# Sums of squares from the feature-major input and the decay chain one block earlier, in a fused transformer block

## The chip, the cores and the metric

The kernel runs on one core of one Trainium2 chip. A time is the device time of one execution in microseconds (us); the profiled execution also has a span, from its first to its last instruction. Weights and activations are float32 in memory.

## What is computed

One block of a hybrid network on 256 tokens of 2048 features: a token mixer (a gated MLP with spatial gating, and a chunked gated linear attention, GLA), cross attention over a memory, and a convolutional feed-forward layer, each with RMS norms around it. What the change touches is the start of the mixer:

```python
def rmsnorm(x, g):
    return x * rsqrt(mean(x * x, -1) + EPS) * g
h = rmsnorm(x, pre_norm_mix)
z_sg, q, k, v, og, g_lr, m_a, m_b = split(h @ w_in)
u, vs = split(gelu(z_sg), 2)
y_a = spatial_gating(u, layernorm(vs, sg_ln_g, sg_ln_b), sg_w, sg_b)
gate_logit = g_lr @ gla_w_gate2 + gla_b_gate
log_a = maximum(log_sigmoid(gate_logit) / 16, -1)
bcum = cumsum(log_a)                  # in chunks of 64 tokens
q_in, k_in = q * exp(bcum), k * exp(-bcum)
```

## The kernel before

**Products in high and low parts.** A float32 operand is split into a high part, a cast on ScalarE (`split_half`, L89), and a low part, a subtraction on VectorE (L90); TensorE multiplies high by high, low by high and high by low. Weights arrive in tiles of 1 MB (`raw`, three buffers, loaded from SP's queue) and are split in pieces of 128 x 1024; there are four buffers of high and four of low parts, so TensorE can have at most four pieces ahead. In a block with tokens on the output's partitions (`tok_block`, L117) a piece feeds 12 matmuls of 512 columns; with features there (`feat_block`, L143), 8 of 512 and 8 of 256. The products accumulate in PSUM, with six tiles tagged `mm` and two tagged `aux`.

**Order.** Most of the kernel is ordered by a scheduler that works on a simulated time line and takes instructions roughly in program order where they are ready. Inside `tc.manual_schedule` the order is as written. The list `later` holds small pieces of work; `tok_block` runs one of them after each piece but the first, `feat_block` after each piece (`step`), and `flush` runs the rest.

**The first projection** (L399 to L453) is written out by hand. It multiplies the input `xT`, which is in memory feature-major (features on partitions), with the second half of the spatial gating's weights, in eight units of two feature blocks. A unit takes 24 matmuls. For each unit the input is scaled by the norm's gain and split (`gain_x`, L372), the weights are split, and TensorE runs. The factor rstd of each token is applied behind the product, so it is needed only when the projection's result leaves PSUM.

**Sums of squares.** For rstd the token-major rows of x are loaded as well, in eight pieces of 128 x 512 (`load_x`, L357), squared on ScalarE with a sum (`square_x`, L362, L366), summed on VectorE, and raised to the power -1/2 on POOL (`rstd_of`, L150). `row_bcast` (L176) multiplies the identity by rstd and puts a row of it on all partitions with two matmuls (`rbc`).

**Low-rank gate.** Sixteen matmuls with the rank-16 weights (L452) follow, then ScalarE and VectorE make `glr` of the result (L455 to L462).

**After that.** `sg_v` takes the first projection out of PSUM with a Gelu (L467), and layer norm over it (L476 to L483) runs on VectorE. Then come two blocks of the projection for `u` (`tok_block`, L549 and L552, matmuls at L106 to L108) with a Gelu each (`sg_u`, L470). Within the first, `gate` (L493) runs four times with two matmuls each, and `decay` (L503): absolute value, Exp, Ln and subtractions. Within the second, `cums` (L509) runs a scan along the tokens and builds exponents, and `powers` (L528) makes two exponentials for each of four heads; `powers` for heads 1 to 3 stand in the q and k blocks (L582). Those (L579 to L603, matmuls at L137 to L141) use the powers on VectorE behind their products; `gating` (L533, matmuls `sps` at L537) uses layer norm's result and `u`.

Of the kernel before, what the change touches and what calls it, by code (L numbers as in the profile page):

```python
# [11 lines left out]
F32 = mybir.dt.float32  # L12
F32R = mybir.dt.float32r
AF = mybir.ActivationFunctionType
# [3 lines left out]
P = 128  # L18
# [6 lines left out]
H = 4  # L25
# [19 lines left out]
def block_kernel(ctx: ExitStack, tc: tile.TileContext, a, out):  # L45
# [269 lines left out]
    with ExitStack() as mix:  # L315
# [20 lines left out]
        with ExitStack() as st2:  # L336
            xp0 = pool(st2, "sp0", side="right")

            gmix = xp0.tile([P, KD], F32, name="gmix")
            xt = [xp0.tile([P, 2, S], F32, name=f"xt_{i}") for i in range(KD // 2)]  # L340
            wgr = xp0.tile([P, KD, 16], F32, name="glr_raw")
            wg = xp0.tile([P, KD, 5, 16], F32R, name="wg")
            gl1 = xp0.tile([80, S], F32, name="gl1")
            gh1 = xp0.tile([48, S], F32R, name="gh1")
            g2 = uu[1][0:96, :]
            xh, ss4s, rs = {}, {}, []

            def load_xt(k, n, eng=nc.sync):
                eng.dma_start(out=xt[k // 2][:, k % 2:k % 2 + n, :], in_=a["xT"][:, k:k + n, :])

# [5 lines left out]

            def load_x(i):  # L357
                t, n = divmod(i, 4)
                xh[i] = xp0.tile([P, 512], F32, tag="xh", bufs=3, name=f"x0_{t}_{n}")
                nc.sync.dma_start(out=xh[i], in_=a["x"][t * P:(t + 1) * P, n * 512:(n + 1) * 512])  # L360

            def square_x(i):  # L362
                t, n = divmod(i, 4)
                if n == 0:
                    ss4s[t] = stat.tile([P, 4], F32, tag="ss4", name=f"ss4_mix_{t}")
                nc.scalar.activation(out=uu[0][:, 0:512], in_=xh[i], func=AF.Square, accum_out=ss4s[t][:, n:n + 1])  # L366
                if n == 3:
                    ss = stat.tile([P, 1], F32, tag="ss", name=f"ss_mix_{t}")
                    nc.vector.reduce_sum(out=ss, in_=ss4s[t], axis=AX.X)
                    rs.append(rstd_of(ss, 1.0 / D, f"mix_{t}", const.tile([P, 1], F32, name=f"r_mix_{t}")))  # L370

            def gain_x(k):  # L372
                split_psum(hT[:, k, 0, :], hT[:, k, 1, :], xt[k // 2][:, k % 2, :], scale=gmix[:, k:k + 1])

            def later_loads(i):
                if i == 3:
                    nc.sync.dma_start(out=ident, in_=a["eye"])
# [6 lines left out]
                if i == 4:  # L384
                    nc.sync.dma_start(out=wgr, in_=a["w_glr"])
                    nc.sync.dma_start(out=g2, in_=a["gate2"])
                if i == 6:
# [5 lines left out]
                    nc.vector.tensor_tensor(out=gate2[64:96, :], in0=g2[64:96, :], in1=gate2[64:96, :].bitcast(F32),  # L393
                                            op=ALU.subtract)
                    nc.sync.dma_start(out=lng, in_=a["sg_ln_g"].partition_broadcast(P))
                if i == 7:
                    nc.sync.dma_start(out=lnb, in_=a["sg_ln_b"].partition_broadcast(P))

            first = []  # L399
            with tc.manual_schedule():  # L400
# [12 lines left out]
                pss = [[mm_psum(f"sg_{n}_{t}") for t in range(NT)] for n in (2, 3)]  # L413
                nx = 0
                for i in range(KD // 2):
                    if 1 <= i < KD // 2 - 2:
                        load_xt(2 * i + 4, 2)
                        load_unit()
# [17 lines left out]
                    for j in sorted(xh):  # L436
                        if j >= nx:
                            square_x(j)
                    nx = len(xh)
                    for j in {2: (0, 1), 3: (2,), 4: (3, 4), 5: (5,), 6: (6, 7)}.get(i, ()):  # L440
                        load_x(j)
                    later_loads(i)
                    for k in (2 * i, 2 * i + 1):
                        c = slice(k % 2 * 512, (k % 2 + 1) * 512)
                        for n, (hi, lo) in enumerate(hl):
                            for j, (part, w) in enumerate(((0, hi), (1, hi), (0, lo))):
                                for t in range(NT):
                                    nc.tensor.matmul(pss[n][t], hT[:, k, part, t * P:(t + 1) * P], w[:, c],
                                                     start=k == 0 and j == 0, stop=k == KD - 1 and j == 2)
                ps = mm_psum("glr")  # L450
                for k in range(KD):
# [22 lines left out]
        for n, ps in enumerate(pss):  # L474
            sg_v(ps, n + 2)
        for t in range(NT):  # L476
            mv = stat.tile([P, 2], F32, tag="mv", name=f"mv_{t}")
# [7 lines left out]
        with ExitStack() as st2:  # L485
# [5 lines left out]
            nc.gpsimd.memset(keep[:, :, 0:1], 0.0)  # L491

            def gate(i):  # L493
                gps = aux_psum(f"gate_{i}")
                for j in range(2):
# [4 lines left out]
                nc.scalar.activation(out=la[:, 2 * i:2 * i + 2, :], in_=gv, func=AF.Abs)  # L500
                nc.vector.tensor_scalar_min(mn[:, 2 * i:2 * i + 2, :], gv, 0.0)

            def decay():  # L503
                nc.scalar.activation(out=la, in_=la, func=AF.Exp, scale=-1.0)
                nc.scalar.activation(out=la, in_=la, func=AF.Ln, bias=1.0)
                nc.vector.tensor_tensor(out=la, in0=mn, in1=la, op=ALU.subtract)
                nc.vector.tensor_scalar(out=la, in0=la, scalar1=1.0 / 16.0, scalar2=-1.0, op0=ALU.mult, op1=ALU.max)
# [39 lines left out]

            later += [partial(gate, i) for i in range(4)] + [decay]
            sg_u(tok_block(a["w_sg"], 0, hT, KD, "sg"), 0)  # L549
            flush()  # L550
            later += [cums, partial(powers, 0)]
            ps = tok_block(a["w_sg"], 1, hT, KD, "sg")  # L552
# [8 lines left out]
        with ExitStack() as st:  # L561
# [454 lines left out]
```

## Time and profile before

| what | value |
|---|---|
| three runs, median | 1662.66 us (1661.40 to 1663.66) |
| the profiled execution, its own time | 1661.93 us |
| its span | 1660.20 us |
| TensorE busy | 1646.9 us |
| VectorE busy | 1042.1 us |
| ScalarE busy | 846.1 us |
| mean granted TensorE clock | 0.999 |

Rows of a timeline give the start, the busy time, the engine (PE is TensorE, ACT ScalarE, DVE VectorE, SP the engine that issues most transfers), the line of the kernel, the operation, its output and inputs, shapes and a count; in brackets stands the idle time before it and what ended it. The end of a matmul is modelled: its busy time overlaps the next one's, so starts are to be compared, not busy times. One float32 matmul counts as two records.

### The profile page before, as it was taken

The page shows a single profiled execution, that of the slowest core. Times are in us where ns is not written, and L with a number is a line of the kernel's source. Part 1 is how long each engine was busy: PE and PEld are TensorE (multiplying, and loading weights), DVE is VectorE, ACT ScalarE, POOL GpSimd, SP SyncE. Part 2 cuts the span into 40 slices and gives each one's busy share as a digit, 9 for nine tenths or more (in the row PEclk, how much of TensorE's full clock was granted, in tenths as well). Part 3 has the DMA queues.
Part 4 walks back from the last instruction along what each step waited for, and adds up shares of the span by engine and source line. Part 5 has one row for each costly group of instructions (what it writes and reads, how often), then busy time and mean ns, then how long its engine had stood idle before and what let it go on. Part 6 is the DMA issues. An engine that isn't in the chain of part 4 may idle for free.

```text
span 1660.2 us, 20835 instructions
## 1 busy us (share of the span) xinstructions
PE 1646.9 (99%) x8086; PEld 1374.8 (83%) x8086; DVE 1042.1 (63%) x1394; ACT 846.1 (51%) x1182; POOL 39.8 (2%) x128
## 2 busy tenths in 40 slices
PE   9999999999999999999999999999999999999998
PEld 7788888888888888888888888888888888888886
DVE  5777645555454545465766877877777787444444
ACT  6774444444444444455655756555555555344332
POOL 0100000000000000000002000000000000000000
PEclk9999999999999999999999999999999999999999
DMA  9545455445555554585542555555555555555553
GB/s 344 221 160 177 177 186 172 176 176 177 186 194 178 182 198 178 187 333 215 204 177 105 202 193 187 181 200 178 190 191 182 195 181 216 190 187 193 179 199 103
DMA packets 49139, 317.52 MB, mean 191 GB/s; under 512 B 5552, under 2 KB 6192, under 8 KB 12304
## 3 DMA queue, kind: packets, MB, share of 16 engines
q1 hardware_dynamic: 48752, 315.93, 53.4%
q8 instruction: 63, 1.03, 0.2%
q14 instruction: 36, 0.29, 0.1%
q10 hardware_dynamic: 288, 0.27, 0.0%
HBM read 314.08 MB, written 2.10 MB: 190 GB/s over the span
## 4 chain that ended last, share of the span: by engine, by line
PE 95%; DMA 2%; ACT 1%; issue 1%; DVE 1%; SPq 0%; DVEq 0%; POOLq 0%; POOL 0%; ACTq 0%
PE up L137 18%; PE up L138 10%; PE ffn L108 5%; PE ffn L107 5%; PE ffn L106 5%; PE m L108 4%; PE m L107 4%; PE m L106 4%; PE p L108 3%; PE p L106 3%; PE p L107 3%; PE mix L108 2%; PE mix L106 2%; PE og L107 2%; PE v L108 2%; PE og L106 2%
## 5 line engine op out<-in xcount | busy, mean ns | idle before, releaser
L90 DVE TENSOR_TENSOR lo<-raw,hi 128x1024 fp32r<-128x1024 f32 (+1 forms) x567 | 689.5, 1219 | 460.9 <-ACT hi L89 456.7
L89 ACT CAST hi<-raw 128x1024 fp32r<-128x1024 f32 (+1 forms) x568 | 590.5, 1043 | 534.4 <-PE ffn L107 133.6
L137 PE MATMUL up<-fT,hi 128*128 128x512 f32 x1320 | 467.3, 394 | 0.4 <-DVE fT L210 0.4
L138 PE MATMUL up<-fT,lo 128*128 128x256 f32 x1320 | 373.1, 283 | 0.0
L137 PEld LDWEIGHTS up<-fT,hi 128*128 128x128 f32 x1320 | 247.9, 188 | 54.3 <-DVE fT L210 0.7
L138 PEld LDWEIGHTS up<-fT,lo 128*128 128x128 f32 x1320 | 248.1, 188 | 3.9
L108 PE MATMUL ffn<-lo,act 128*128 128x512 f32 x352 | 140.1, 399 | 0.0
L107 PE MATMUL ffn<-hi,act 128*128 128x512 f32 x352 | 138.7, 394 | 0.0
L106 PE MATMUL ffn<-hi,act 128*128 128x512 f32 x352 | 138.0, 392 | 0.0
L893 ACT COPY hd<-up 128x256 f32<-128x256 f32 x88 | 32.7, 373 | 137.0 <-PE up L141 137.0
L106 PE MATMUL m<-hi,hT 128*128 128x512 f32 x256 | 101.4, 396 | 0.0
L108 PE MATMUL m<-lo,hT 128*128 128x512 f32 x256 | 101.3, 396 | 0.0
L107 PE MATMUL m<-hi,hT 128*128 128x512 f32 x256 | 101.1, 395 | 0.0
L894 DVE TENSOR_TENSOR hd<-up,hd 128x256 f32<-128x256 f32 x88 | 37.4, 425 | 72.4 <-ACT hd L893 72.4
L107 PEld LDWEIGHTS ffn<-hi,act 128*128 128x128 f32 x352 | 66.1, 188 | 17.2
L106 PEld LDWEIGHTS ffn<-hi,act 128*128 128x128 f32 x352 | 66.1, 188 | 15.7
L108 PEld LDWEIGHTS ffn<-lo,act 128*128 128x128 f32 x352 | 66.1, 188 | 15.3
L107 PEld LDWEIGHTS m<-hi,hT 128*128 128x128 f32 x256 | 48.1, 188 | 11.4
L108 PEld LDWEIGHTS m<-lo,hT 128*128 128x128 f32 x256 | 48.1, 188 | 11.4
L106 PEld LDWEIGHTS m<-hi,hT 128*128 128x128 f32 x256 | 48.1, 188 | 11.2
L897 ACT ACTIVATE cv<-hd,cols 128x256 f32<-128x256 f32 x88 | 52.7, 602 | 0.3
L106 PE MATMUL v<-hi,hT 128*128 128x512 f32 x128 | 51.1, 399 | 0.0
(301 smaller groups left out, 2480.1 us busy)
## 6 DMA issues: line engine op xcount, KB each, us to landing
raw<-in_w_up SPq DMA_DIRECT2D x88, 1024.0 KB, 4.8
raw<-in_w_dn SPq DMA_DIRECT2D x44, 1024.0 KB, 4.8
raw<-in_w_v SPq DMA_DIRECT2D x16, 1024.0 KB, 4.8
raw<-in_w_og SPq DMA_DIRECT2D x16, 1024.0 KB, 4.8
raw<-in_w_ma SPq DMA_DIRECT2D x16, 1024.0 KB, 4.8
raw<-in_w_mb SPq DMA_DIRECT2D x16, 1024.0 KB, 4.8
raw<-in_w_pb SPq DMA_DIRECT2D x16, 1024.0 KB, 4.8
raw<-in_w_o SPq DMA_DIRECT2D x16, 1024.0 KB, 4.9
```

The costliest lines, as they stand in the source:

```text
L89: nc.scalar.copy(out=hi, in_=raw)
L90: (eng or nc.vector).tensor_tensor(out=lo, in0=raw, in1=hi.bitcast(F32), op=ALU.subtract)
L106: nc.tensor.matmul(ps, xh, wh, start=first, stop=False)
L107: nc.tensor.matmul(ps, xl, wh, start=False, stop=False)
L108: nc.tensor.matmul(ps, xh, wl, start=False, stop=last)
L137: nc.tensor.matmul(*big, start=k == 0, stop=False)
L138: nc.tensor.matmul(*small, start=False, stop=False)
L893: nc.scalar.copy(out=hd[:, 2:], in_=ps[:, S:2 * S])
L894: nc.vector.tensor_tensor(out=hd[:, 2:], in0=ps[:, 0:S], in1=hd[:, 2:], op=ALU.add)
L897: nc.scalar.activation(out=cv, in_=hd[:, 2:], func=AF.Identity, scale=cols[:, w0 + 2:w0 + 3], bias=cols[:, C_CB + j:C_CB + j + 1])
```

## The change

- The eight loads of token rows go. Squares are taken of `xT` itself, two feature blocks at a time, and added up on VectorE into `acc`; at the last feature block the two halves are added, and two matmuls with `acc` as the stationary operand and two columns of ones give each token's sum on its partition (`token_rstd`). One operation on VectorE and one power on POOL make both columns of rstd.
- `xT` lies in one tile; from the loop it is loaded in transfers of four, four and two feature blocks instead of two each.
- The rank-16 weights and the gate's weights are loaded a unit earlier and cast a unit earlier, identity and columns are loaded a unit later.
- Layer norm moves from before the first `u` block into the second.
- The four `gate` steps run in one, behind the third piece of the first `u` block, with PSUM tiles of the `mm` kind, and hold them until `decay`; the minimum with zero is fused into the subtraction. `decay`, `cums` and all four `powers` follow in the first block; TensorE's order in that block is as written.

```diff
-            xt = [xp0.tile([P, 2, S], F32, name=f"xt_{i}") for i in range(KD // 2)]
+            xt = xp0.tile([P, KD, S], F32, name="xt")
+            acc = xp0.tile([P, 2, S], F32, name="acc")
...
-            def load_x(i):
...
-                nc.sync.dma_start(out=xh[i], in_=a["x"][t * P:(t + 1) * P, n * 512:(n + 1) * 512])
...
             def square_x(i):
...
-                nc.scalar.activation(out=uu[0][:, 0:512], in_=xh[i], func=AF.Square, accum_out=ss4s[t][:, n:n + 1])
...
+                sq = acc if i == 0 else xp0.tile([P, 2, S], F32, tag="sq", bufs=2, name="sq")
+                nc.scalar.activation(out=sq, in_=xt[:, 2 * i:2 * i + 2, :], func=AF.Square)
+                if i > 0:
+                    nc.vector.tensor_tensor(out=acc, in0=acc, in1=sq, op=ALU.add)
+
+            def token_rstd():
+                nc.vector.tensor_tensor(out=acc[:, 0, :], in0=acc[:, 0, :], in1=acc[:, 1, :], op=ALU.add)
+                tot = aux_psum("tot")
+                for t in range(NT):
+                    nc.tensor.matmul(tot[:, 2 * t:2 * t + 2], acc[:, 0, t * P:(t + 1) * P], ones[:, 0:2],
+                                     start=True, stop=True)
+                ms = stat.tile([P, NT], F32, tag="ms2", name="ms_mix")
+                nc.vector.tensor_scalar(out=ms, in0=tot[:, 0:2 * NT:2], scalar1=1.0 / D, scalar2=EPS,
+                                        op0=ALU.mult, op1=ALU.add)
+                nc.gpsimd.tensor_tensor(out=rr, in0=ms, in1=neg_half, op=ALU.pow)
...
                     if 1 <= i < KD // 2 - 2:
-                        load_xt(2 * i + 4, 2)
+                        if i % 2:
+                            load_xt(2 * i + 4, min(4, KD - 2 * i - 4))
                         load_unit()
...
-                    for j in {2: (0, 1), 3: (2,), 4: (3, 4), 5: (5,), 6: (6, 7)}.get(i, ()):
-                        load_x(j)
+                    square_x(i)
                     later_loads(i)
                     for k in (2 * i, 2 * i + 1):
+                        if k == KD - 1:
+                            token_rstd()
...
-        for t in range(NT):
+        def layer_norm(t):
...
             def gate(i):
-                gps = aux_psum(f"gate_{i}")
+                gps = mm_psum(f"gate_{i}")
...
-                nc.vector.tensor_scalar_min(mn[:, 2 * i:2 * i + 2, :], gv, 0.0)
+                gvs.append(gv)
 
             def decay():
                 nc.scalar.activation(out=la, in_=la, func=AF.Exp, scale=-1.0)
                 nc.scalar.activation(out=la, in_=la, func=AF.Ln, bias=1.0)
-                nc.vector.tensor_tensor(out=la, in0=mn, in1=la, op=ALU.subtract)
+                for i, gv in enumerate(gvs):
+                    part = la[:, 2 * i:2 * i + 2, :]
+                    nc.vector.scalar_tensor_tensor(out=part, in0=gv, scalar=0.0, in1=part, op0=ALU.min, op1=ALU.subtract)
...
-            later += [partial(gate, i) for i in range(4)] + [decay]
-            sg_u(tok_block(a["w_sg"], 0, hT, KD, "sg"), 0)
+            def gates():
+                for i in range(4):
+                    gate(i)
+
+            later += [lambda: None, gates, decay, cums] + [partial(powers, q) for q in range(H)]
+            with tc.manual_schedule(engines={mybir.EngineType.PE}):
+                ps = tok_block(a["w_sg"], 0, hT, KD, "sg")
             flush()
-            later += [cums, partial(powers, 0)]
+            sg_u(ps, 0)
+            later += [partial(layer_norm, t) for t in range(NT)]
             ps = tok_block(a["w_sg"], 1, hT, KD, "sg")
...
-                if h < H - 1:
-                    later.insert(0, partial(powers, h + 1))
```

## Rows read from the trace of the kernel before

**Rows 1.** The page's first part: busy us, share of the span, instructions

```profile
PE 1646.9 (99%) x8086; PEld 1374.8 (83%) x8086; DVE 1042.1 (63%) x1394; ACT 846.1 (51%) x1182; POOL 39.8 (2%) x128
```

**Rows 2.** TensorE's timeline, first projection, two starts 26 repeats apart

```profile
7.96 1.09 PE L448 MATMUL sg<-hi,hT 128*128 128x512 f32 x4
...
44.36 1.09 PE L448 MATMUL sg<-hi,hT 128*128 128x512 f32 x4
```

**Rows 3.** TensorE's timeline, the last unit of the first projection

```profile
45.29 0.63 PE L448 MATMUL sg<-lo,hT 128*128 128x512 f32 x2
46.24 1.19 PE L448 MATMUL sg<-hi,hT 128*128 128x512 f32 x4 [0.32 <-ACT hi L89]
47.79 0.73 PE L448 MATMUL sg<-lo,hT 128*128 128x512 f32 x2 [0.36 <-DVE lo L90]
48.36 1.09 PE L448 MATMUL sg<-hi,hT 128*128 128x512 f32 x4
```

**Rows 4.** TensorE's timeline, end of the second u block and first q block

```profile
100.47 0.40 PE L107 MATMUL sg<-hi,hT 128*128 128x512 f32 x1
101.07 0.51 PE L108 MATMUL sg<-lo,hT 128*128 128x512 f32 x1 [0.20 <-DVE lo L90]
101.41 0.39 PE L106 MATMUL sg<-hi,hT 128*128 128x512 f32 x1
...
112.30 1.05 PE L537 MATMUL sps<-vv,sgw 128*128 128x128 f32 x8
113.78 0.49 PE L137 MATMUL q<-hT,hi 128*128 128x512 f32 x1 [0.42 <-ACT hi L89]
115.03 0.39 PE L138 MATMUL q<-hT,lo 128*128 128x256 f32 x1 [0.76 <-DVE lo L90]
115.26 0.39 PE L137 MATMUL q<-hT,hi 128*128 128x512 f32 x1
```

**Rows 5.** ScalarE to 56 us: a wait (total, times, longest), a timeline row

```profile
ACT uu L366 <- DMA x<-in_x: 8.6, 5, 2.6
...
45.15 3.88 ACT L89 CAST hi<-raw 128x1024 fp32r<-128x1024 f32 x4
```

**Rows 6.** VectorE's timeline: the scan

```profile
95.48 4.42 DVE L510 TENSOR_TENSOR_SCAN mn<-keep,la 128x2048 f32<-128x2048 f32 x1
```

**Rows 7.** ScalarE's timeline from the Ln to the casts of the q block

```profile
86.78 1.92 ACT L505 ACTIVATE la<-la 128x2048 f32<-128x2048 f32 x1
...
102.56 1.28 ACT L530 ACT_TABLE_LOAD   x1
...
105.95 1.03 ACT L89 CAST hi<-raw 128x1024 fp32r<-128x1024 f32 x1
106.89 3.90 ACT L531 ACTIVATE E<-E 128x1024 f32<-128x1024 f32 x4
110.81 1.28 ACT L472 ACT_TABLE_LOAD   x1
...
112.69 1.03 ACT L89 CAST hi<-raw 128x1024 fp32r<-128x1024 f32 x1
```

**Rows 8.** Groups of one shape to 126 us: busy us, mean ns | idle before

```profile
L366 ACT ACTIVATE uu<-x 128x512 f32<-128x512 f32 x8 | 5.1, 632 | 8.7 <-DMA x<-in_x 8.6
L90 DVE TENSOR_TENSOR lo<-raw,hi 128x1024 fp32r<-128x1024 f32 x37 | 44.2, 1220 | 15.2 <-ACT hi L89 15.1
L501 DVE TENSOR_SCALAR mn<-gate 128x512 f32<-128x512 f32 x4 | 2.7, 687 | 1.4 <-ACT la L500 1.4
L506 DVE TENSOR_TENSOR la<-mn,la 128x2048 f32<-128x2048 f32 x1 | 2.3, 2293 | 2.6 <-ACT la L505 2.6
```

**Rows 9.** Busy time by stretch: length, PE, PEld, DVE, ACT, POOL, clock, DMA

```profile
6.15:45.52 39.37, 39.37 (x168) 31.71 (x168) 24.93 (x35) 26.63 (x50) 1.65 (x2) 1.00 1.02 376
```

**Rows 10.** Timeline: the first u block's first matmul, the last step to glr

```profile
56.40 0.48 PE L106 MATMUL sg<-hi,hT 128*128 128x512 f32 x1
...
65.66 0.41 DVE L462 TENSOR_TENSOR glr<-gl,gh 16x256 fp32r<-16x256 f32 x1
```

More of the change, by code (lines that the diff above doesn't have):

```diff
@@ L344, in block_kernel @@
             gh1 = xp0.tile([48, S], F32R, name="gh1")
+            rr = const.tile([P, NT], F32, name="r_mix")
+            rs = [rr[:, t:t + 1] for t in range(NT)]
             g2 = uu[1][0:96, :]
-            xh, ss4s, rs = {}, {}, []
             def load_xt(k, n, eng=nc.sync):
-                eng.dma_start(out=xt[k // 2][:, k % 2:k % 2 + n, :], in_=a["xT"][:, k:k + n, :])
+                eng.dma_start(out=xt[:, k:k + n, :], in_=a["xT"][:, k:k + n, :])
             def load_unit(parts=((slice(0, 2), slice(0, 2)),)):
@@ L355, in load_unit @@
                     nc.sync.dma_start(out=first[i][:, n, k, :], in_=a["w_sgv"][i, :, n, k, :])
-            def load_x(i):
-                t, n = divmod(i, 4)
-                xh[i] = xp0.tile([P, 512], F32, tag="xh", bufs=3, name=f"x0_{t}_{n}")
-                nc.sync.dma_start(out=xh[i], in_=a["x"][t * P:(t + 1) * P, n * 512:(n + 1) * 512])
             def square_x(i):
-                t, n = divmod(i, 4)
-                if n == 0:
-                    ss4s[t] = stat.tile([P, 4], F32, tag="ss4", name=f"ss4_mix_{t}")
-                nc.scalar.activation(out=uu[0][:, 0:512], in_=xh[i], func=AF.Square, accum_out=ss4s[t][:, n:n + 1])
[L367 to L370, printed above, removed]
+                sq = acc if i == 0 else xp0.tile([P, 2, S], F32, tag="sq", bufs=2, name="sq")
@@ L372, in gain_x @@
             def gain_x(k):
-                split_psum(hT[:, k, 0, :], hT[:, k, 1, :], xt[k // 2][:, k % 2, :], scale=gmix[:, k:k + 1])
+                split_psum(hT[:, k, 0, :], hT[:, k, 1, :], xt[:, k, :], scale=gmix[:, k:k + 1])
             def later_loads(i):
                 if i == 3:
+                    nc.sync.dma_start(out=wgr, in_=a["w_glr"])
+                    nc.sync.dma_start(out=g2, in_=a["gate2"])
+                if i == 4:
                     nc.sync.dma_start(out=ident, in_=a["eye"])
@@ L383, in later_loads @@
                         fill=0.0, base=0, channel_multiplier=-1)
[L384 to L387, printed above, removed]
                     for j in range(5):
@@ L394, in later_loads @@
                                             op=ALU.subtract)
+                if i == 6:
                     nc.sync.dma_start(out=lng, in_=a["sg_ln_g"].partition_broadcast(P))
@@ L413, in block_kernel @@
                 pss = [[mm_psum(f"sg_{n}_{t}") for t in range(NT)] for n in (2, 3)]
-                nx = 0
                 for i in range(KD // 2):
                     if 1 <= i < KD // 2 - 2:
-                        load_xt(2 * i + 4, 2)
+                        if i % 2:
+                            load_xt(2 * i + 4, min(4, KD - 2 * i - 4))
                         load_unit()
@@ L435, in block_kernel @@
                             split_half(first[i][:, n, :, :].rearrange("p k c -> p (k c)"), into=x)
[L436 to L439, printed above, removed]
-                    for j in {2: (0, 1), 3: (2,), 4: (3, 4), 5: (5,), 6: (6, 7)}.get(i, ()):
-                        load_x(j)
+                    square_x(i)
                     later_loads(i)
                     for k in (2 * i, 2 * i + 1):
+                        if k == KD - 1:
+                            token_rstd()
                         c = slice(k % 2 * 512, (k % 2 + 1) * 512)
@@ L491, in block_kernel @@
             nc.gpsimd.memset(keep[:, :, 0:1], 0.0)
+            gvs = []
             def gate(i):
-                gps = aux_psum(f"gate_{i}")
+                gps = mm_psum(f"gate_{i}")
                 for j in range(2):
```

## The prediction

> **What bounds the kernel now.** I read the page's busy shares first: TensorE is busy for 1646.9 of 1660.2 us [rows 1], so only a stop of TensorE, or work added to it, can move the end. A busy share hides short stops, because the end of a matmul is modelled, so I went on with start times in TensorE's timeline. From 7.96 to 44.36 us the first projection runs 26 repeats of six matmuls of 512 columns, 156 in 36.40 us, one each 0.233 us [rows 2]. That is the pace. Wherever two starts are further apart, the rest is a stop.
>
> Three places in the part that the change touches are off the pace. In the last unit of the first projection, two matmuls start at 45.29 and the next at 46.24, where two paces end at 45.76: 0.48. Four from 46.24 should end at 47.17 and the next starts at 47.79: 0.62. The two from there lose 0.10 more before 48.36. Together 1.20 us [rows 3]. Near the end of the second gating-projection block 0.60 and 0.34 stand where 0.233 should, 0.48 us [rows 4]. In the first q block eight passes of 0.111 from 112.30 end at 113.19, the next starts at 113.78 (0.59); the next waits until 115.03 (1.02 over the pace); the one after that starts 0.23 later where 0.12 is usual for 256 columns (0.11): 1.72 us [rows 4]. **All there is to win is 1.20 + 0.48 + 1.72 = 3.40 us**, 0.20% of the time.
>
> Whose fault is each? The first: ScalarE was held up by token rows, five waits with 8.6 us in all, the longest 2.6, and it came to the casts of the last unit only at 45.15 [rows 5], 0.6 before TensorE wanted them. The second: the scan keeps VectorE from 95.48 to 99.90, and the low part that TensorE waits for stands behind it [rows 6]. The third: after ScalarE's table load at 102.56 come the powers (two exponentials for each of four heads), up to 110.79, with a single cast among them, then a Gelu table, a Gelu, and the next cast at 112.69 [rows 7]; by then TensorE has used up its four buffers of high and low parts.
>
> **The change, part by part.**
>
> *Sums of squares.* Eight squares of token rows (0.63 each, and a read of the sum) [rows 8] become eight squares of the same 512 elements per partition taken from data that is there for the projection anyway. The wait for token rows goes, and with it eight transfers of 256 KB on SP's queue; the xT loads become three on that queue from the loop instead of five, with the same bytes, and the rank-16 weights are queued a unit earlier, the identity and the columns a unit later. VectorE gets seven additions of 512 elements, taken at 0.69 each like the minima of that shape [rows 8], and one of 256, at most as much: 5.5 us. VectorE is busy 24.9 of 39.4 us and ScalarE 26.6 in that stretch [rows 9], so both fit: 0. Were that cover gone, the last additions would stand before the two-column products, whose place in TensorE's fixed order is half a unit (12 matmuls, 2.8 us) behind the start of the last unit; two additions of 1.1 us fit there too. The stop of 1.20 us should go: the last unit's casts then wait only for weights and for the buffers of unit 5, which TensorE leaves two dozen paces before 45.76, at 40.2; two casts and a low part later is 43.5. What is late next is the last unit's weight load, one unit ahead of its need. I take -1.20; the ends are -1.20 and 0.
>
> *Two two-column products* are new work for TensorE: float32, so two passes each, each with its own 128-column weights. No row has two columns. From above, four weight loads that nothing covers, at the mean of all weight loads, 1374.8 / 8086 = 0.17 [rows 1]: 0.7; from below, two columns of 512 in each pass at the pace, so next to 0. The nearest in kind are the 128x128 passes of the gating, 0.111 each with a fresh weight load [rows 4]. I take 4 x 0.11 = +0.44.
>
> *Rstd.* One multiply-add and one power of two columns instead of two of one: off TensorE. On POOL's queue it stands behind the mask of the gating weights, as the second power does now, and the diagonals are wanted only 16 low-rank matmuls (3.7 us) after the projection. 0; if it came later than that, row_bcast would hold TensorE by as much, since its place there is fixed.
>
> *Decay chain, VectorE.* Four minima of 0.69 and a subtraction of 2.29 [rows 8] become four fused ones on PSUM, taken at the 0.69 of the minima: 2.3 us less on VectorE, none of it TensorE's. Only the casts' wait for ScalarE and VectorE can show it: see the last term.
>
> *Decay chain, order.* All four gate products stand behind the third of eight pieces, 36 matmuls or 8.4 us into the block; the eight passes cost what they cost now. They need the low-rank input, ready now at 65.66 + 0.41 = 66.07, 9.67 us after the block's start at 56.40 [rows 10]. Layer norm, which is between on VectorE now, moves to the second block, so I take it as in time (0; the upper end is 9.67 - 8.4 = 1.3 us). The gates' four PSUM tiles are now of the six that projections use, held until the fused minima; the next block needs two of them some 14 us after the gates. Abs (4 x 0.63, as the squares of 512 elements [rows 8]), two table loads (1.28), Exp and Ln (1.92 each, by the row of the Ln [rows 7]) and two minima make 2.5 + 2.6 + 3.8 + 1.4 = 10.3: in time by about 4, with room for three casts. 0.
>
> *Where the two later stops go.* The Gelu of the next block, which stands behind the powers now, with its table load takes ScalarE from 110.81 to 112.69, 1.9 us, about what that bunch cost TensorE; with the powers a block earlier it no longer falls there. So both old stops, -0.48 and -1.72, go. But the scan (4.42) and the powers (102.56 to 110.79, 8.2 with one cast [rows 7]) are still each in one place, and now before the casts in program order, so one may still beat the four-piece lead. **I take +0.75 for new stops**, one like the scan's 0.48 and a half of another. The lower end is 0; the upper is worked out below.
>
> Sum: -1.20 + 0.44 - 0.48 - 1.72 + 0.75 = **-2.2 us**. The profiled execution took 1661.93 us, its span 1660.20, and is 0.73 below the median of the runs, 1662.66. So 1659.7 on its own time, and on the median **1660.4 us**.
>
> By the Trainium skill, page "ScalarE: Activation LUTs", section "Table sets: the hidden batching unit", a logarithm and then an exponential need one table load, since one set holds both. The trace speaks against it here: the Ln has run from 86.78, and the exponentials at 102.56 took a load of their own [rows 7], with only casts and copies between.
>
> **The rivals.**
>
> *Slower: VectorE starves the low parts.* The chain now comes ahead of the second block's splits in program order, and layer norm next to them. TensorE lives on four buffered pieces of 2.8 us; a cast can begin when a piece is left and must be done, low part too, 8.4 us later, so an engine may be away 8.4 - 1.03 - 1.22 = 6.1 us [rows 7, 8]. Four fused minima (2.75), the scan (4.42) and layer norm's six passes of 1024 elements (at most 1.22 each, 7.3) in one go are 14.5: 8.4 us of stop. Against the certain -2.96 that is +5.4: **1668.1**. It decides from 6.3 us of new stops on. For it: the scan alone made a stop already [rows 4, 6]. Against: low parts slip in wherever the chain waits for its own result, layer norm can fill the time before the Ln is there, and the chain is 2.3 us shorter on VectorE.
>
> *No gain.* The same without layer norm: minima, the scaling (at most the 2.29 of the subtraction) and the scan are 9.5, which is 3.4 us of stop: +0.4, **1663.1**. The late input of the gates (1.3) with a stop of 1.7 comes to the same.
>
> *Clean: no new stop.* -3.40 + 0.44 = -2.96, or -3.3 with the products near 0.1: 1659.7 or 1659.4, say **1659.5**, at the edge of 0.2%. One way there is the shared table: with Exp, Ln and the powers on one load ScalarE would be 2 x 1.28 us freer [rows 7], and the 0.75 would be 0. That is the rule cited above; its share of this chance is small, as the row denies it.
>
> *The first stop stays* (another input, such as the last xT load, holds ScalarE instead): -2.2 + 1.2 = -1.0, **1661.7**. Against it: token rows are the cause that the wait names.
>
> **How the numbers follow.** Likeliest 0.60; clean 0.14; first stop stays 0.08; no gain 0.08; slower 0.10. Bounds of the unknown terms spread the likeliest by -0.8 and +1.5, runs scatter by 1.1. Range 1658.6 to 1664.4, which leaves out most of the slower case and a little below. About 0.2% (3.3 us) is what a measurement of this kernel can tell from no change. Faster by more needs the clean case with cheap products and a little scatter: 0.10. Slower by more: 0.10. Within: 0.80.
>
> **What would show it.** Right: no wait of ScalarE for token rows, the last unit of the first projection at the 0.233 pace; four short passes before its last 12 matmuls, costing about 0.44; the gates in one run of eight with no gap ahead; at most about one us of stops where the scan and the exponentials stand. Wrong: a gap ahead of the gates, or of the second block's first matmul (PSUM held), or stops of over 2 us on a cast or low part in the second block.

## The result: 20 us faster, and nearly all of it where no step looked

The changed kernel takes **1641.95 us** (median of 4, 1641.45 to 1642.91) against 1662.16 before (4 runs of the same comparison); the ratio is 0.9881, 95% interval 0.9866 to 0.9895. Forecast were 1660.4, range 1658.6 to 1664.4, with 0.80 on "within 0.2%" and 0.10 on faster. It is 20 us faster, six times all the stops that the prediction had found. The profiled execution of the changed kernel took 1642.16, its span 1640.5.

First the places that the prediction spoke of. The page's first part of the changed kernel (busy us, share, instructions; answers to [rows 1]), then TensorE's timeline at the end of the first projection and in the second u block (answer to [rows 3] and [rows 4]):

```profile
PE 1628.3 (99%) x8090; PEld 1372.4 (84%) x8090; DVE 1044.1 (64%) x1398; ACT 845.9 (52%) x1174; POOL 40.0 (2%) x127
```

```profile
46.83 1.07 PE L449 MATMUL sg<-hi,hT 128*128 128x512 f32 x4
47.74 0.61 PE L449 MATMUL sg<-lo,hT 128*128 128x512 f32 x2
48.19 0.50 PE L369 MATMUL tot<-ones,acc 128*128 128x2 f32 x4
48.55 0.93 PE L449 MATMUL sg<-hi,hT 128*128 128x512 f32 x3
...
92.70 0.39 PE L107 MATMUL sg<-hi,hT 128*128 128x512 f32 x1
92.93 0.40 PE L106 MATMUL sg<-hi,hT 128*128 128x512 f32 x1
93.62 0.50 PE L108 MATMUL sg<-lo,hT 128*128 128x512 f32 x1 [0.29 <-DVE lo L90]
```

The stop in the last unit is gone, the four passes of the two-column products take 0.36, and a new stop of about half a microsecond stands in the second u block (another, early in the first projection, is taken up below). That is as forecast, and it is worth some 2 us, not 20. TensorE is busy for 18.6 us less, with four passes more. So its single matmuls must follow each other faster. The timeline at 270 us shows it, first before, then after (both are blocks of `tok_block` on the same `hT`, matmul by matmul):

```profile
270.04 0.40 PE L108 MATMUL v<-lo,hT 128*128 128x512 f32 x1
...
271.44 0.40 PE L108 MATMUL v<-lo,hT 128*128 128x512 f32 x1
```

```profile
270.09 0.39 PE L107 MATMUL og<-hi,hT 128*128 128x512 f32 x1
...
271.45 0.39 PE L107 MATMUL og<-hi,hT 128*128 128x512 f32 x1
```

Six matmuls lie between the two starts of each fence: 1.40 us before, 0.233 each; 1.36 after, 0.227 each. Nothing waits, the shapes are the same, the granted clock is 1.00 in both. The window view counts it over 100 us of the up block (features on the output's partitions) and of the feed-forward block that follows (columns: stretch, length, PE busy with its instructions, PEld, DVE, ACT, POOL, clock, DMA share, GB/s), first before, then after:

```profile
1100.00:1200.00 100.00, 100.00 (x571) 87.63 (x570) 79.09 (x126) 58.74 (x90) 1.78 (x18) 1.00 0.54 190
1500.00:1600.00 100.00, 100.00 (x431) 80.43 (x430) 46.01 (x45) 40.27 (x44) 0.00 (x0) 1.00 0.53 186
```

```profile
1100.00:1200.00 100.00, 100.00 (x567) 86.72 (x566) 78.49 (x125) 58.24 (x90) 1.81 (x18) 1.00 0.54 190
1500.00:1600.00 100.00, 100.00 (x439) 82.04 (x438) 46.87 (x44) 41.27 (x45) 0.00 (x0) 1.00 0.54 194
```

In the feed-forward block 439 matmuls fit where 431 did; in the up block 567 where 571 did, so that one has become **slower**. Neither block is named in the diff. The table sums it over the kernel; a spacing is the mean distance of neighbouring starts in the trace, those over 0.3 us left out, and for blocks with features on the output's partitions that of a pair (512 and 256 columns).

| blocks | count | spacing before, ns | after, ns | worth, us |
|---|---|---|---|---|
| sg, v, og, m, p (`tok_block` on hT, yaT, ybT) | 2496 | 232.9 to 233.1 | 226.7 to 227.5 | -15.1 |
| mix, ffn (`tok_block` on mT, act) | 1440 | 233.3 | 229.0 | -6.3 |
| xv (`tok_block` on fT) | 96 | 232.7 | 228.2 | -0.4 |
| up (pairs) | 1408 | 350.8 | 353.3 | +3.5 |
| k, q, xk, xq (pairs) | 384 | 347.5 to 353.4 | 352.5 to 353.2 | +0.3 |

Sum -18.0 us, of a difference of 19.7 between the spans; 1.7 is left for the stops. What the matmuls have in common is where their operands lie in on-chip memory, and the diff does move that (all addresses here are those of the compiled programs). The two const tiles `r_mix_0` and `r_mix_1`, each rounded up to 32 bytes per partition, became one of 32: everything allocated behind, the weight buffers `raw`, `hi` and `lo` first, starts 32 bytes lower. The new tag `ms2` in the pool `stat`, four buffers of 32 bytes, adds 128: hT, yaT, ybT and fT, behind both, start 96 bytes higher. mT, act and h2T are allocated from the other end and stay.

### The profile page after: what moved, and what is told of

It reads as the page before. It is cut to its first block, busy times and chain, and to the rows that moved or that the text cites. A ratio compares the mean times of both kernels' runs of the same rounds, so it can differ in the third digit from the quotient of the medians.

```text
span 1640.5 us, 20820 instructions
## 1 busy us (share of the span) xinstructions
PE 1628.3 (99%) x8090; PEld 1372.4 (84%) x8090; DVE 1044.1 (64%) x1398; ACT 845.9 (52%) x1174; POOL 40.0 (2%) x127
## 4 chain that ended last, share of the span: by engine, by line
PE 96%; ACT 1%; DVE 1%; DMA 1%; issue 1%; SPq 0%; DVEq 0%; POOLq 0%; POOL 0%; ACTq 0%
PE up L137 19%; PE up L138 10%; PE ffn L106 5%; PE ffn L108 5%; PE ffn L107 5%; PE m L107 4%; PE m L106 4%; PE m L108 4%; PE p L107 3%; PE p L106 3%; PE p L108 3%; PE sg L449 2%; PE mix L108 2%; PE mix L107 2%; PE v L107 2%; PE v L108 2%
```

## The experiments

In what follows D is the start of the stationary operand less the start of the moving one, in bytes per partition, modulo 256. In `tok_block` the activations are stationary and the weights' 512 columns move; in `feat_block` it is the other way round. All steps inside these tiles are multiples of 512 bytes, so one D holds for a whole block. Before, D was 128 on hT, yaT and ybT, 160 on mT and act, 128 for up; after, 0, 192 and 0.

**e1, e2: the same shift in both kernels.** In the changed kernel, and in the kernel before:

```diff
-    neg_half = const.tile([P, 2], F32, name="neg_half")
+    neg_half = const.tile([P, 10], F32, name="neg_half")
```

(in e1 the one use of the whole tile takes its first two columns). 

> The changed kernel with one constant tile 32 bytes larger, so that the weight buffers (raw, high, low) start at a multiple of 64 bytes again, as before the change, and so do hT, yaT, ybT and fT; the order of the instructions on TensorE, VectorE, ScalarE and SP is that of the changed kernel. Placement theory (the 32-byte shift of the operands set TensorE's pace): 512-column matmuls of the token blocks go back from 0.227 to 0.233 us, the time to about 1660 us; what is left against before, some -1.5 us, is what the change's own steps bring. Rival (the new order, the missing token rows or the moved decay chain made the pace): the pace stays 0.227 and the time 1642 us.

> The kernel before with one constant tile 32 bytes larger, so that the weight buffers and hT, yaT, ybT, fT start 32 bytes past a multiple of 64; nothing else differs, and the order on TensorE, VectorE, ScalarE and SP is the same. Placement theory: the token blocks run at 0.227 us per 512-column matmul instead of 0.233, the feature blocks about 2 ns per pair slower, together some -18 us: 1643 to 1646 us, with the three stops of before (3.4 us) still there. Rival: 0.233 and 1662 us.

Measured: e1 1647.74 us, ratio 0.9918 (0.9905 to 0.9932), 5.8 more than the changed kernel; e2 1659.32, 0.9985 (0.9976 to 0.9994), 2.5 less than its before. Neither time is one that the theory or the rival had forecast. Thirty-two unused bytes move the time by 5.8 and 2.5 us; all the work that the diff edits will turn out to be worth 2.7 (e5). In e1 the weights and hT move together, so D on hT stays 0, and v, og and m keep their 226.7 to 227.4 ns; mT and act stay, D there goes from 192 back to 160, and mix and ffn go from 229.0 back to 233.3 (1440 x 4.3 ns = 6.2 us). In e2, too, D on hT stays, at 128; on mT and act it goes from 160 to 128, and mix and ffn from 233.3 to 232.4. The window view of e1:

```profile
1100.00:1200.00 100.00, 100.00 (x568) 86.73 (x567) 78.56 (x125) 58.10 (x89) 1.79 (x18) 1.00 0.53 187
1500.00:1600.00 100.00, 100.00 (x430) 80.47 (x429) 46.20 (x44) 40.23 (x44) 0.00 (x0) 1.00 0.54 189
```

The feed-forward count is that of before, 430, the up count that of after. So the start of the weights alone doesn't set the pace, nor does that of the activations: hT moved without effect, act lay still and changed.

**e3, e4: the activations moved alone.** e4 is the kernel before, e3 that of e2, each with 32 more bytes between the weights and hT:

```diff
+    nc.gpsimd.memset(stat.tile([P, 8], F32, tag="gap", bufs=1, name="gap"), 0.0)
```

> The kernel before with the weight buffers alone 32 bytes past a multiple of 64 and hT, yaT, ybT, fT at a multiple of 64 (a constant tile 32 bytes larger and a 32-byte tile behind the weight buffers). If the moving operand's start decides: token blocks (weights moving) at 0.227, time near that of both shifted, 1644 us. If the stationary one's decides: token blocks on hT, yaT and ybT stay at 0.233, and only blocks with weights stationary (q, k, up) change. If both must be shifted: 0.233 there, and 0.229 only where the stationary operand lies 32 bytes off anyway (mix, ffn). Rival (nothing to do with placement): 1662 us.

> The kernel before with the weight buffers where they were (a multiple of 64) and hT, yaT, ybT, fT 32 bytes past one. If the moving operand decides: token blocks stay at 0.233 and the time near 1662 us, or a little off through q, k and up, where hT and fT move. If the stationary one decides: token blocks on hT, yaT, ybT go to 0.227, while mix and ffn, whose stationary operand has not moved, stay at 0.233: about 1650 us. Rival (nothing to do with placement): 1662 us and no change in any block.

Measured: e3 1655.20 us, 0.9964 (0.9951 to 0.9978); e4 1656.03, 0.9969 (0.9956 to 0.9981). On hT both have D = 160, and stay at 233.3 to 233.4 ns: the fast place is not just any other place. But for up D is now 96, and a pair takes 347.3 instead of 350.8 (1408 x 3.5 ns = 4.9), most of the gain of both runs (6.6 and 5.8 us). Taken alone, e3 looks as if the start of the stationary operand decided, since only the blocks with stationary weights got faster by much, and e4 as if that of the moving one did; no theory of one operand fits both. e4's window, for up:

```profile
1100.00:1200.00 100.00, 100.00 (x577) 87.92 (x576) 80.00 (x126) 59.35 (x90) 1.79 (x18) 1.00 0.53 190
```

**e5, e6: program and places exchanged.** e5 is the changed program with the weight buffers and the activations where they lay before; e6 is the program of before, in the same order on every engine, with those operands where the changed kernel has them. (Tiles of a few dozen small matmuls, the rank-16 weights among them, lie elsewhere.)

```diff
 e5, from the changed kernel:
-    neg_half = const.tile([P, 2], F32, name="neg_half")
+    neg_half = const.tile([P, 10], F32, name="neg_half")
-                ms = stat.tile([P, NT], F32, tag="ms2", name="ms_mix")
+                ms = stat.tile([P, NT], F32, tag="mv", name="ms_mix")
 e6, from the kernel before:
-            xh, ss4s, rs = {}, {}, []
+            xh, ss4s, rs = {}, {}, []; rr = const.tile([P, NT], F32, name="r_mix")
-                    rs.append(rstd_of(ss, 1.0 / D, f"mix_{t}", const.tile([P, 1], F32, name=f"r_mix_{t}")))
+                    rs.append(rstd_of(ss, 1.0 / D, f"mix_{t}", rr[:, t:t + 1]))
-            dg = stat.tile([P, P], F32, tag="dg", bufs=2, name=f"dg_{name}_{t}")
+            dg = stat.tile([P, P + 16], F32, tag="dg", bufs=2, name=f"dg_{name}_{t}")[:, 0:P]
```

> The changed program with every weight buffer and every stationary or moving tile of the matmuls at the byte address that it has in the kernel before (a constant tile 32 bytes larger, one small statistics tile sharing a slot). New theory, from the first four runs: the pace depends on the distance between the start of the stationary and of the moving operand, modulo 256 bytes (0 in the changed kernel, 128 before). Then the pace is that of before, 0.233, and the time shows what the change's own steps bring: 1662 less about 1.5, 1660 to 1661 us. Rival (the change's steps bring the bulk, e.g. by missing token rows): below 1655 us.

> The program before, instruction by instruction, with those tiles at the byte addresses of the changed kernel (the two rstd columns in one constant tile, 32 bytes less; a statistics tile 128 bytes larger in all). Distance theory: the changed kernel's pace in every block, 0.227 in the token blocks and 0.229 in mix and ffn, which is 18.5 us less by the two traces: 1643 to 1645 us, with the three stops of before still there. Rival (steps, not places): 1662 us.

Measured: e5 **1659.21 us**, ratio 0.9985 (0.9976 to 0.9994); e6 **1644.62**, ratio 0.9899 (0.9885 to 0.9913). e6 is in its forecast, e5 0.8 us under its own. With the two kernels themselves, and e9 and e10 below (from several comparisons, in which the median of the kernel before lay between 1661.43 and 1662.16):

| medians, us | places of before | places of after | best places found |
|---|---|---|---|
| program of before | 1661.95 | 1644.62 | 1633.55 |
| program of after | 1659.21 | 1641.95 | 1630.15 |
| the program's worth | -2.7 | -2.7 | -3.4 |

The places are worth 17.3 us with either program, the program 2.7 at either of the first two places. **That is what the change is: 2.7 us of edits (1.0 to 4.0 by the interval of e5), and 17.3 of a memory plan that moved by 32 and 96 bytes.** e6, which has nothing of the change, has the counts of the changed kernel:

```profile
1100.00:1200.00 100.00, 100.00 (x568) 86.72 (x568) 79.12 (x124) 57.69 (x88) 1.79 (x18) 1.00 0.52 183
1500.00:1600.00 100.00, 100.00 (x439) 82.06 (x438) 47.63 (x45) 40.53 (x45) 0.00 (x0) 1.00 0.54 192
```

**e7, e8: other distances.** From the changed kernel, each activation tile through a helper that puts j x 32 unused bytes ahead of it (`lead`) or behind:

```diff
+    def moved(p, j, n, name, lead=True):
+        t = p.tile([P, n * NT * S + 8 * j], F32R, name=name)
+        o = 8 * j if lead else 0
+        return t[:, o:o + n * NT * S].rearrange("p (k h s) -> p k h s", h=NT, s=S)
-        hT = mp.tile([P, KD, NT, S], F32R, name="hT")
+        hT = moved(mp, 0, KD, "hT")
...
```

with j = 0, 1, 1, 3, 3, 7, 7 for hT, yaT, ybT, mT, fT, h2T, act in e7, and 7, 6, 1, 14, 2, 5, 6 in e8. 

> The changed kernel with some tiles moved by multiples of 32 bytes, so that blocks run at different distances (stationary start minus moving start, modulo 256): token blocks on hT 0, on yaT 32, on ybT 64, mix 96, xv 96, ffn 224; feature blocks k and q 0, xk and up 160, xq 32. Distance theory: hT blocks stay at 0.227, k and q at 353 ns a pair; mix and xv, both 96, agree with each other; ffn, whose block alone was between at 192, has a new value. If the start of one operand alone counts, the weights' start has not moved and every token block stays at 0.227.

> As the run before, with other distances: token blocks on hT 224, on yaT 160, on ybT 192, mix 0 (also modulo 512), xv 64, ffn 0 (256 modulo 512); feature blocks k and q 32, xk and up 192, xq 224. Distance theory: token blocks at 160 are back at 0.2333, at 192 at 0.229, mix and ffn at 0.227 whichever of 0 and 256 it is modulo 512; hT blocks equal the ffn block of the run before (224), xv equals ybT there (64), k and q equal xq there (32). Rival (one operand's start alone, or the position of a tile in memory): these pairs differ.

Measured, one execution each: e7 1649.08 us, e8 1650.38. Their use is the table of spacings, over all ten kernels so far and e9 below (og, m, p, mix, ffn and up, xk, xq; in sg, v, k and q there are stops among the matmuls):

| D | 512 columns, `tok_block`, ns | pair of 512 and 256, `feat_block`, ns |
|---|---|---|
| 0 | 226.7 to 227.2 | 353.2 to 353.9 |
| 32 | 233.2 | 352.3 |
| 64 | 233.3 | 352.5 |
| 96 | 234.2 | 347.3 to 349.0 |
| 128 | 232.3 to 233.1 | 350.8 to 351.7 |
| 160 | 233.3 to 233.4 | 350.5 to 352.1 |
| 192 | 228.9 to 229.0, or 231.2 | 351.4 to 352.3 |
| 224 | 233.3 to 233.4 | 348.0 |

One figure sorts the `tok_block` work, whatever its tile, with one exception: at 192, mix and ffn (distance 448 modulo 512) took 229.0 and the p block on ybT (192 modulo 512) 231.2, where e8's expectation had 229, so modulo 256 is not all of it. For pairs it sets 96 and 224 apart as the fastest and 0 as the slowest; the ranges between overlap. (xk takes up to 1.6 ns more a pair than up at the same D, and xv, 96 matmuls, ran at 228.2 at D = 0.) The two kinds of block want different distances: 0 is the best for `tok_block` and the worst for `feat_block`.

**e9, e10: the table used as a forecast.** The changed program (e9) and that of before in the places of e6 (e10), both with the helper and j = 0, 0, 0, 6, 5, 1, 6: D is 0 for all `tok_block` work on hT, yaT, ybT, mT and act, and 96 for up, xk and xq. Instruction order is that of the parent kernel on every engine.

> The changed kernel with mT and act moved by 192 bytes down, h2T by 32 and fT by 160 up, so that every block's distance between stationary and moving start, modulo 256 bytes, is one that was fast in the runs so far: 0 for all blocks with 512 token columns on mT, act (now 192), and 96 for the feature blocks on fT and h2T (now 0). Instructions, their order and their waits stay. Theory (the distance sets the pace): mix and ffn at 226.7 ns instead of 229.0 (1440 matmuls, -3.3 us), up at 347.4 a pair instead of 353.3 (1408 pairs, -8.3), xk and xq at 347.4 instead of 352.5 (128 pairs, -0.7), xv at 233.3 instead of 229.0 (96, +0.4): 11.9 us less than 1641.95, about 1630. Rival (the pace of the large up block is held by the weights' casts or loads, and the 353 was chance): 1638 to 1642, with stops of TensorE in the up block in place of the longer pace.

> The program of before in the places of the changed kernel (as in e6_old_program_changed_places, 1644.6), with the same four tiles moved as in e9_changed_program_best_places. Theory: places and program add: 1644.6 - 11.9 = 1632.7, and the difference to e9 is what the program of the change is worth, 2.7 us as at the old places. Rival (at a faster TensorE the stops of the old program grow, since casts, scan and exponentials keep their lengths): the difference is 4 us or more.

Measured: e9 **1630.15 us** (1629.96 to 1630.39), ratio 0.9812 (0.9799 to 0.9826); e10 **1633.55**, 0.9832 (0.9819 to 0.9845). The table gave 1630 for e9. Spacings: mix 226.9, ffn 226.7, a pair of up 347.4. e9 is the fastest version of the study, 31.3 us under before. Its windows:

```profile
1100.00:1200.00 100.00, 100.00 (x578) 87.91 (x577) 79.87 (x127) 59.35 (x90) 1.79 (x18) 1.00 0.53 190
1500.00:1600.00 100.00, 100.00 (x443) 82.84 (x442) 47.54 (x45) 41.38 (x45) 0.00 (x0) 1.00 0.55 195
```

The program is worth 3.4 here instead of 2.7, and e10 came out 0.9 over its forecast. Its timeline, where [rows 3] and [rows 4] stand for the same stops before (its lines are five further down, by the helper):

```profile
44.31 0.61 PE L453 MATMUL sg<-lo,hT 128*128 128x512 f32 x2
45.76 1.20 PE L453 MATMUL sg<-hi,hT 128*128 128x512 f32 x4 [0.83 <-ACT hi L94]
47.32 0.73 PE L453 MATMUL sg<-lo,hT 128*128 128x512 f32 x2 [0.37 <-DVE lo L95]
...
98.90 0.39 PE L112 MATMUL sg<-hi,hT 128*128 128x512 f32 x1
100.08 0.50 PE L113 MATMUL sg<-lo,hT 128*128 128x512 f32 x1 [0.80 <-DVE lo L95]
```

Behind 44.31 two matmuls need 0.45 of the 1.45 us to the next; 1.0 is lost, where [rows 3] have 0.48. But this first stop varies from execution to execution, as the section on the prediction shows. The wait behind the scan varies less: it costs 0.95 at 98.90, and 1.05 with its remnant, in e10 as in e6, where it was 0.37 with a remnant of 0.11 before (0.33 to 0.43 in e2, e3 and e4). A faster TensorE comes sooner to a low part that is no earlier. What makes the 0.7 us is not settled: e6 alone ran from 1644.11 to 1647.04, and at the places of before e5 gave 0.6 back in the up block, as the section on the prediction shows.

**e11, e12: the halves of the program, at the places of before.** e11 has the decay chain alone (the diff from `layer_norm` on), e12 the sums of squares alone (the diff up to there, with e5's two edits that keep the places).

```diff
 e11, from the kernel before:
-        for t in range(NT):
+        def layer_norm(t):
...
-            later += [partial(gate, i) for i in range(4)] + [decay]
+            later += [lambda: None, gates, decay, cums] + [partial(powers, q) for q in range(H)]
...
 e12, from the kernel before:
-            def load_x(i):
...
+            def token_rstd():
...
```

> The kernel before with only the second half of the change: gates in one group, fused minima, the decay chain within the first gating block, layer norm after it; token rows are still read for the sums of squares, and all operands of TensorE lie where they lay before. Theory (the steps of the prediction, new stops at 0 as seen in e5): the stops of 0.48 and 1.72 us go, the 1.20 in the last unit of the first projection stays and no two-column products are added: 1661.95 - 2.2 = 1659.8. Rival (the stops move rather than go, and the gain of e5 was the first stop's): 1661 to 1662, with new stops of 1.5 to 2 us in the first or second gating block.

> The kernel before with only the first half of the change: squares of the feature-major input, two-column products, one power, loads a unit earlier or later; the decay chain and the gates stay where they were, and all operands of TensorE lie where they lay before. Theory (the halves stand for separate stops, as the prediction added them): the first stop goes and the two-column products cost 0.36 to 0.44 us, while the stops of about 0.5 and 1.7 us near 100 and 113 us stay; since the first stop was 1.2 us in the trace of before, but 0.15 to 1.7 us in other executions of its program, 0.3 to 1.3 us less than before, about 1661. Rival (the halves need each other: in e11, with the decay chain alone, a new stop of 0.7 us stood before the spatial products, which waited for layer norm): the gain is over 1.3 us already here, or there is none, with a new stop.

Measured: e11 1659.85 us, 1.6 under its before (1661.43; ratio 0.9992, 0.9984 to 1.0001); e12 1661.02, 1.1 under its before (1662.10; 0.9994, 0.9985 to 1.0003). Neither ratio alone tells its kernel from the one before; the two medians together make the 2.7 of e5. In e11 the two stops of [rows 4] are gone, and one of 0.7 stands elsewhere (TensorE, then the last step to the gates' input in e11 and in e5):

```profile
63.61 0.40 PE L108 MATMUL sg<-lo,hT 128*128 128x512 f32 x1
64.55 1.13 PE L541 MATMUL sps<-vv,sgw 128*128 128x128 f32 x8 [0.54 <-DVE vv L483]
...
64.43 0.41 DVE L462 TENSOR_TENSOR glr<-gl,gh 16x256 fp32r<-16x256 f32 x1
...
59.92 0.42 DVE L464 TENSOR_TENSOR glr<-gl,gh 16x256 fp32r<-16x256 f32 x1
```

The spatial products come ahead of the gates here and wait for layer norm. The gates could not have gone first: their input is ready only at 64.84, 1.0 us behind the pace, so the late input that the prediction priced at up to 1.3 is there without the first half of the change. In e5, which has both halves, it is ready at 60.34 and the stop isn't there. In e12 the last unit of the first projection runs without a stop, and the stops of 0.48 and 1.72 us gave way to some at other places that lose about as much (from 95 to 108 us, 2.0 in all). So the halves add in time, within the noise, but not because each owns its stops.

## Why the prediction was wrong

**The step that failed is the first one: "one each 0.233 us [rows 2]. That is the pace."** From it came the bound "All there is to win is 1.20 + 0.48 + 1.72 = 3.40 us". 0.233 was measured, but as a property of the engine, when it was one of the layout: the same matmul takes 0.227 us at another distance between its operands. A bound made of stops alone holds only as long as the work between them is fixed, and the prediction never asked whether the spacing of matmuls of one shape was the same in all blocks of the trace. It was not: the 64 xq pairs of before ran at 347.5 ns where those of up took 350.8. Its own sign of being right, "the last unit of the first projection at the 0.233 pace", failed on this: in the changed kernel four matmuls take 0.91 there (46.83 to 47.74), 0.227 each.

**The edit whose price was missed is the one taken at 0.** Under "Rstd" the prediction costed one tile of two columns in place of two of one as instructions, and the new statistics tile not at all. As instructions they cost nothing, as it said; as allocations they were worth -17.3 us. No rival had this case.

**The working of the edits themselves held.** At equal places (e5) the time is 2.7 us less, against the 2.2 of the sum, inside its range; the case "clean", 1659.5 with a chance of 0.14, is what e5 gave (1659.21). That it comes so near is in part luck. TensorE's first v matmul, the first of up and the first of ffn, before and then in e5:

```profile
204.02 0.48 PE L106 MATMUL v<-hi,hT 128*128 128x512 f32 x1
...
908.41 0.50 PE L137 MATMUL up<-fT,hi 128*128 128x512 f32 x1
...
1405.37 0.40 PE L106 MATMUL ffn<-hi,act 128*128 128x512 f32 x1
```

```profile
200.54 0.48 PE L106 MATMUL v<-hi,hT 128*128 128x512 f32 x1
...
904.95 0.50 PE L137 MATMUL up<-fT,hi 128*128 128x512 f32 x1
...
1402.46 0.39 PE L106 MATMUL ffn<-hi,act 128*128 128x512 f32 x1
```

At v, behind all that the change touches, e5 is 3.5 us ahead; the up block takes 497.51 us in e5 and 496.96 before and gives 0.6 of it back, at the same D. Why is not shown. Term by term, by e5's timeline:

```profile
47.77 0.62 PE L449 MATMUL sg<-lo,hT 128*128 128x512 f32 x2
48.23 0.50 PE L369 MATMUL tot<-ones,acc 128*128 128x2 f32 x4
48.59 1.18 PE L449 MATMUL sg<-hi,hT 128*128 128x512 f32 x4
...
63.75 0.40 PE L108 MATMUL sg<-lo,hT 128*128 128x512 f32 x1
63.99 1.11 PE L501 MATMUL gate<-glr,gate 96*128 96x256 f32 x8
64.94 0.40 PE L106 MATMUL sg<-hi,hT 128*128 128x512 f32 x1
```

- *First stop, -1.20.* It is gone in e5. But its size was one execution's: in e2 the same program lost 0.4 us there, in e4 1.6, in e11, which keeps the token rows, 0.1. None of the seven traces without token rows has the stop. e12's 1.1, products included, is the only figure for that half alone, and its interval doesn't exclude nothing. The waits for token rows themselves went, and ScalarE now waits for weights, as "what is late next" said; the waits of ScalarE up to 56 us in the changed kernel (total, times, longest; answer to [rows 5]):

```profile
ACT hi L89 <- DMA raw<-in_w_sgv: 8.2, 7, 2.6
ACT hi L89 <- PE sg L449: 3.7, 2, 3.4
ACT hi L89 <- DVE acc L366: 3.0, 1, 3.0
```

  The last row puts a cast behind the final addition of the squares, which the prediction took as costing nothing; TensorE doesn't stop for it.

- *Two-column products, +0.44.* Four passes take 0.36 (48.23 to 48.59), and the matmul behind them starts its successor 0.08 late (the group's 1.18 for 1.09): 0.44, a lucky hit to the hundredth.
- *Squares and their additions, 0.* Seven additions of 0.684 us and one of 0.425 (the estimate was 0.69), all done by 43.0, 5.3 us before the products.
- *Gates, 0, with 1.3 as the upper end.* They run as eight without a gap. Their input is ready at 60.34 in e5, 4.8 us after the block's first matmul at 55.54. The bound took the 9.67 of before over unchanged, and e11, at 64.84, shows that it was no idle worry. The reason given for 0, layer norm's move to the second block, is half right: in e5 layer norm still runs in the first block, but two of its six passes instead of five come ahead of the gates' input.
- *Later stops, -0.48 and -1.72, and +0.75 for new ones.* Both are gone in e5, and no new one came: +0.75 was too much at the old pace. In the changed kernel itself two appear. One of 0.7 us at 92.93 (fence in the section on the result; the low part behind the scan and the exponentials) goes with the faster TensorE: e1, e7 and e9, with hT at the fast spacing, have it as well, e5 and e8 do not. In e5 the same low part, started at 92.64 (92.34 in the changed kernel), was just in time. The other, 0.9 us from 17 to 19 us, differs between executions: casts wait for weights there, and e12 loses 1.0 at the old pace, e9 0.3, e1 0.1. The changed kernel's ScalarE and TensorE, then e12's TensorE:

```profile
16.67 2.00 ACT L89 CAST hi<-raw 128x1024 fp32r<-128x1024 f32 x2 [1.80 <-DMA raw<-in_w_sgv]
17.77 1.20 PE L449 MATMUL sg<-hi,hT 128*128 128x512 f32 x4 [0.29 <-ACT hi L89]
...
18.33 1.20 PE L449 MATMUL sg<-hi,hT 128*128 128x512 f32 x4 [0.42 <-ACT hi L89]
```

- *Table loads.* Exp and the Ln behind it, with one cast between, still took a load each, so the prediction's reading of [rows 7] stands. The load of the powers' Exp at 87.88 says nothing more, since a Gelu's load came between (76.94). ScalarE's timeline of the changed kernel:

```profile
66.71 1.28 ACT L508 ACT_TABLE_LOAD   x1
68.00 1.92 ACT L508 ACTIVATE la<-la 128x2048 f32<-128x2048 f32 x1
...
70.88 1.28 ACT L509 ACT_TABLE_LOAD   x1
72.17 1.92 ACT L509 ACTIVATE la<-la 128x2048 f32<-128x2048 f32 x1
...
76.94 1.28 ACT L474 ACT_TABLE_LOAD   x1
...
87.88 1.28 ACT L536 ACT_TABLE_LOAD   x1 [0.70 <-DVE E L525]
```

Of the rivals, "VectorE starves the low parts" did not happen: layer norm ran ahead of the Ln, and the scan, 4.42 us at 81.06, let the low parts in before and after it:

```profile
79.93 1.22 DVE L90 TENSOR_TENSOR lo<-raw,hi 128x1024 fp32r<-128x1024 f32 x1
81.06 4.42 DVE L516 TENSOR_TENSOR_SCAN mn<-keep,la 128x2048 f32<-128x2048 f32 x1
85.40 1.20 DVE L90 TENSOR_TENSOR lo<-raw,hi 128x1024 fp32r<-128x1024 f32 x1
```

## What to carry to other kernels

When TensorE is busy from end to end, look at the spacing of its starts by block and shape before calling a spacing the pace; two blocks of one shape at different spacings are a reserve, here 28 us of 1662 with the program of before, eight times its stops. A change that adds, drops or resizes any on-chip tile moves all that is allocated behind it, so compare the memory plans of the two kernels, and measure an edit's own worth with unused bytes that put the operands back. Settle the places last and on purpose, by padding the activations against the weight buffers, since the next edit of a one-column tile may undo them.

## What the runs showed of the hardware

The spacing of float32 matmuls of one shape, each with a fresh 128 x 128 stationary block, depends on the distance between the stationary and the moving start: 226.7 to 234.2 ns for 512 columns, 347.3 to 353.9 for a pair of 512 and 256, at a granted clock of 1.00 throughout. The best distance of one kind of block is the worst of the other, and the distance modulo 256 bytes sorts all blocks of the first kind but one; of the pairs it sorts the fastest and the slowest. Why is not shown. That the load of the next stationary block and the running matmul's reads disturb each other is only argued, from its being a matter of both starts. The Trainium skill, page "TensorE: Matmul & The Clock Gate", section "Step-by-step: what each phase is for", says that loading the next tile's weights doesn't steal read bandwidth from the running matmul. The runs here show that where the one lies to the other changes the spacing by up to 3%, so the two are not independent in every respect.

A faster TensorE also turned cover into stops: with the same work on the other engines, the wait behind the scan grew from 0.48 us [rows 4] to 1.05 in e6 and e10, and the changed program, without a new stop in e5, has one of 0.7 at 92.93 in the changed kernel.
